# A fused transformer layer on one core: a scale for each half of a pair's activations, products reordered, the output projection pipelined and the late sums spread over ten rounds

## Chip, core and metric

The kernel runs on one core of a Trainium2 chip. The core has a matrix engine (TensorE, PE in the rows; its weight loads are PEld), three elementwise engines (VectorE or DVE, ScalarE or ACT, GpSimd or POOL) and a queue processor (SyncE or SP), which issues nearly all DMAs of this kernel in one order. Each engine runs its own instructions in order and waits on semaphores for the others. The metric is the device time of one execution in microseconds, lower is better; the figure compared is the median of several runs.

## The reference, cut to what matters

One layer (DEPTH is 1) on 2048 tokens of width 1024, all in float32:

```
h  = RMSNorm(x) * (1 + scale1(c)) + shift1(c)
u  = h @ W_in                                  # columns split among head groups
A, B = forgetting attention (8 heads x 64), differential attention (4 heads x 128)
x  = x + gate1(c) * (concat(A, B) @ W_out)
h2 = RMSNorm(x) * (1 + scale2(c)) + shift2(c)
x  = x + gate2(c) * ((silu(h2 @ w_gate) * (h2 @ w_up)) @ w_down)     # hidden width 2816
```

## The kernel before, in words

Float32 products are made of three float16 products: each operand is scaled by a power of two and split into a high and a low half (a cast on ACT, then the difference on DVE), and high*high, high*low and low*high are added in PSUM. The scale comes from a maximum over the tile: `absmax` on DVE gives one value per row, `colmax` spreads it over the rows by a small matmul on PE (line 108) and a second DVE maximum, and `pow2` makes scale and inverse in four short DVE instructions.

**First stage.** The 16 blocks of 128 tokens are normalised (`first_norm`), transposed on PE (`first_hT`) and projected. Per block the norm is a square with sum on ACT, an `rsqrt` of two ACT and three DVE instructions on one column, and a scaling on POOL.

**Attention** for eight head groups, with the input projection of the next group between its steps.

**Output projection.** `out_proj(blk)` loads x and the mixed heads of a block, splits them into `mh`, turns them by a DMA transpose into `mT` (two buffers), multiplies (2 x 24 matmuls), adds x and stores the row in DRAM (`x1d`). Blocks 0 to 9 stand between attention steps; blocks 10 to 15 come after the first gate weights were prepared.

**The gated layer.** Tokens are handled in two halves of 1024, hidden units in 11 pairs of 128, so there are 22 rounds `q`. Gate and up products go by a Strassen scheme: seven products (`product`, in the order `ORDER`) for each of gate (w = 0) and up (w = 1), 12 matmuls each (line 1091), 168 in a round. Their right side is one of seven sums of blocks of the normed tokens (`comb(i)`); `BSUM` says which blocks. The sums of the first half of the tokens (pairs 0 to 3) are made by `norm_sum` during the attention. Those of the second half (`jj` = 4 to 7, seven each, 28 in all) are made in rounds 2, 4, 6 and 8: `norm_load` and `norm_row` bring in and norm two rows, and then for each of the seven sums POOL adds (line 984), ACT casts (988), DVE subtracts (989), SP transposes (995) and stores to DRAM (996). Each sum takes one of the three `stage()` buffers, which the `w_down` loads use too.

After a round, `act` (both token halves `th` of the pair, 2048 values in a row) gets one scale in `act_scale`, and `act_split` makes `aT`. The 16 `down` products of round q (6 matmuls each, line 1149, 96 in all) run in round q+1, as `DOWNAT` spreads them over its 14 slots; DVE adds each to x (line 1153). A slot is one product, its downs, and then whatever steps the code put there.

At a product's end the sums of Strassen's scheme are made from PSUM by DVE, POOL and ACT. For the last (`i` = 6, w = 1):

```
V.tensor_tensor(out=tmp, in0=b, in1=tmp, op=ALU.add)                     # 1120
G.tensor_tensor(out=tmp, in0=tmp, in1=dif, op=ALU.add)                   # 1125
G.tensor_tensor(out=act[:, 1, 1], in0=tmp, in1=act[:, 1, 1], op=ALU.mult) # 1126
```

and `act_scale` of the next round waits for it. A scheduler orders the instructions of each engine from this program, so that steps move a few slots against the text.

## Time and profile before

| | |
|---|---|
| runs | 2935.83, 2925.38, 2928.06 us; median 2928.06 |
| profiled execution | 2939.51 us, its span 2937.7 us |
| PE busy | 2728.9 us, 93% of the span |
| DVE, POOL, ACT busy | 72%, 55%, 49% of the span |
| mean granted clock of PE | 0.98 of full speed |

The profiled execution is 11.4 us longer than the median of the runs, so differences worked out from its rows are taken off the median. Rounds are counted on PE by line 1091: each has 168 of its matmuls. Round 1 begins at 1631.83 us, round 3 at 1753.93, round 10 at 2200.66, round 13 at 2387.92 and round 21 at 2845.55.

### The profile page before, as it was taken

What the parts mean: (1) busy time and instruction counts of PE and PEld (TensorE: products, weight loads), DVE (VectorE), ACT (ScalarE), POOL (GpSimd) and SP (SyncE); (2) the same over time, 40 slices, a digit from 0 to 9 for tenths busy, and PEclk for the clock granted to TensorE, in tenths of its full rate; (3) what the DMA queues carried; (4) which work ended last, traced back from release to release, by engine and by line L of the source; (5) the groups of instructions that cost most, each with busy time, mean ns of one, the idle gap of its engine ahead of it and who ended that gap; (6) DMA issues with size and microseconds to landing.
All of it is one profiled execution on the core that took longest, in us unless ns stands there. A gap on an engine that the chain in (4) does not pass through costs nothing.

```text
span 2937.7 us, 49384 instructions
## 1 busy us (share of the span) xinstructions
PE 2728.9 (93%) x18902; PEld 1479.9 (50%) x18902; DVE 2111.3 (72%) x4077; ACT 1441.2 (49%) x2725; POOL 1609.5 (55%) x1392
## 2 busy tenths in 40 slices
PE   5789989899999999999989998899999999999998
PEld 3456656566665655664444343444444444444443
DVE  7786675857758686656744887787878778778775
ACT  4666667666676777786543422333323332233230
POOL 2566666665667787675542645444545444535430
PEclk9899999999999999999999999999999999999999
DMA  6232231322224233234776223224234511112101
GB/s 230 77 82 61 63 73 39 82 53 67 73 50 94 53 105 95 49 103 118 171 196 202 85 68 98 72 79 110 70 108 150 165 59 57 58 52 64 58 22 58
DMA packets 269902, 261.92 MB, mean 89 GB/s; under 512 B 204376, under 2 KB 221144, under 8 KB 263904
## 3 DMA queue, kind: packets, MB, share of 16 engines
q1 hardware_dynamic: 269664, 258.75, 31.0%
q8 instruction: 148, 2.42, 0.4%
q14 instruction: 90, 0.74, 0.1%
HBM read 173.55 MB, written 36.91 MB: 72 GB/s over the span
## 4 chain that ended last, share of the span: by engine, by line
PE 52%; DVE 21%; DMA 12%; POOL 6%; ACT 6%; issue 4%; SPq 0%; POOLq 0%; DVEq 0%; ACTq 0%
PE ps_mx L1149 10%; PE ps_ip L437 10%; PE ps_st L1091 7%; PE ps_pv L1091 6%; DMA stg<-in_w_ada_dram 3%; PE ps_ip L934 3%; DMA stg<-stg 2%; PE ps_mx L1091 2%; PE ps_st L579 2%; DVE t_mxc L548 2%; PE ps_st L580 2%; PE ps_pv L609 2%; PE ps_mx L546 2%; PE ps_pv L608 2%; PE ps_pv L607 2%
## 5 line engine op out<-in xcount | busy, mean ns | idle before, releaser
L593 POOL TENSOR_TENSOR pxs<-pxs 128x512 f16<-128x512 f32 (+3 forms) x640 | 683.3, 1082 | 325.8 <-ACT pxs L590 191.8
L1091 PEld LDWEIGHTS <-mt 128*128 128x128 f16 x3696 | 361.8, 99 | 446.7 <-issue 22.0
L437 PE MATMUL ps_ip<-wbuf,ht 128*128 128x384 f16 (+1 forms) x2952 | 560.6, 332 | 26.1 <-DVE vts L144 13.5
L1149 PE MATMUL ps_mx<-wide,ht 128*128 128x512 f16 x2112 | 505.4, 382 | 11.5 <-ACT ht L139 5.6
L1038 POOL TENSOR_TENSOR pxm<-vts 128x512 f32<-128x512 f32 x220 | 295.7, 1370 | 347.1 <-DMA vts<-in_w_gu_dram 316.3
L585 ACT ACTIVATE pxs<-ps_st,cells 128x512 f32<-128x512 f32 (+3 forms) x640 | 388.7, 619 | 142.5 <-PE ps_st L580 68.9
L437 PEld LDWEIGHTS <-ht 128*128 128x128 f16 x3072 | 295.7, 99 | 243.5 <-issue 46.2
L1091 PE MATMUL ps_st<-ht,mt 128*128 128x512 f16 x1584 | 383.0, 386 | 5.6 <-ACT mt L1094 3.2
L1091 PE MATMUL ps_pv<-ht,mt 128*128 128x512 f16 x1584 | 383.3, 380 | 1.1 <-ACT mt L1096 1.1
L590 ACT ACTIVATE pxs<-pxs 128x512 f16<-128x512 f32 (+3 forms) x640 | 350.7, 565 | 16.4 <-PE ps_pv L609 7.6
L607 PE MATMUL ps_pv<-vts,pxs 128*128 128x129 f16 (+1 forms) x2176 | 342.6, 207 | 4.2 <-DVE os L626 3.1
L608 PE MATMUL ps_pv<-vts,pxs 128*128 128x128 f16 (+1 forms) x2176 | 344.7, 208 | 0.0
L1149 PEld LDWEIGHTS <-ht 128*128 128x128 f16 x2112 | 206.3, 98 | 266.7 <-issue 16.9
L609 PE MATMUL ps_pv<-vts,pxs 128*128 128x129 f16 (+1 forms) x2176 | 325.6, 207 | 9.8 <-POOL pxs L593 8.9
L548 DVE TENSOR_REDUCE t_mxc<-ps_mx 128x1 f32<-128x512 f32 x384 | 256.9, 682 | 93.8 <-PE ps_mx L546 92.0
L1153 DVE SCALAR_TENSOR_TENSOR mt<-ps_mx,t_ai,mt 128x512 f32<-128x512 f32 x352 | 256.6, 743 | 75.5 <-PE ps_mx L1149 75.2
L607 PEld LDWEIGHTS <-pxs 128*128 128x128 f16 x2176 | 208.2, 97 | 56.7 <-ACT pxs L585 3.5
L579 PE MATMUL ps_st<-mt 67*128 67x512 f16 (+7 forms) x640 | 223.8, 350 | 10.4 <-ACT pxs L585 10.2
L609 PEld LDWEIGHTS <-pxs 128*128 128x128 f16 x2176 | 206.8, 99 | 50.0 <-POOL pxs L593 24.3
L608 PEld LDWEIGHTS <-pxs 128*128 128x128 f16 x2176 | 208.0, 97 | 35.3 <-issue 4.1
L580 PE MATMUL ps_st<-mt 128*128 128x512 f16 (+3 forms) x640 | 223.8, 350 | 0.0
L546 PE MATMUL ps_mx<-mt 71*128 71x512 f16 (+7 forms) x640 | 197.3, 350 | 19.6 <-DVE t_mxc L548 13.1
(266 smaller groups left out, 4097.0 us busy)
## 6 DMA issues: line engine op xcount, KB each, us to landing
vts<-in_w_gu_dram SPq DMA_DIRECT2D x44, 1024.0 KB
stg<-in_w_down_dram SPq DMA_DIRECT2D x44, 512.0 KB
stg<-in_w_ada_dram SPq DMA_DIRECT2D x32, 512.0 KB
stg<-in_w_in_dram SPq DMA_DIRECT2D x24, 512.0 KB
mt<-in_w_ada_dram SPq DMA_DIRECT2D x16, 512.0 KB
mt<-mt SPq DMA_DIRECT2D x128, 64.0 KB
mixed<-os SPq DMA_DIRECT2D x32, 256.0 KB
stg<-in_w_out_dram SPq DMA_DIRECT2D x16, 512.0 KB
```

The costliest lines, as they stand in the source:

```text
L437: T.matmul(pt[:, 0:N], lhsT=h4[:, k, hs, c : c + P], rhs=w4[k // 4][:, k % 4, ws, 0:N], start=(i == 0), stop=(i == len(terms) - 1))
L548: V.tensor_reduce(out=mx[:, 4 * j + n : 4 * j + n + 1], in_=b[:, 0:w], op=ALU.max, axis=AX.X)
L579: T.matmul(b[:, c0:QC], lhsT=K2[0:K, kb * P : (kb + 1) * P], rhs=QA[0:K, q0:q1], start=True, stop=False, skip_group_check=True)
L585: A.activation(p32[:, c0:QC], b[:, c0:QC], AF.Exp, bias=pshift, scale=1.0)
L590: A.activation(ph[:, c0:QC], p32[:, c0:QC], AF.Copy, bias=0.0, scale=1.0)
L593: (V if hilo[1] == "V" else G).tensor_tensor(out=pl[:, c0:QC], in0=p32[:, c0:QC], in1=ph[:, c0:QC], op=ALU.subtract)
L607: T.matmul(pv[:, jj, :], lhsT=lhs_h, rhs=v4[:, kb, h, 0 : W + 1], start=first, stop=False, skip_group_check=True)
L608: T.matmul(pv[:, jj, 0:W], lhsT=lhs_h, rhs=v4[:, kb, h, W + 2 : 2 * W + 2], start=False, stop=False, skip_group_check=True)
L609: T.matmul(pv[:, jj, :], lhsT=lhs_l, rhs=v4[:, kb, h, 0 : W + 1], start=False, stop=end, skip_group_check=True)
L1038: G.tensor_tensor(out=sums[:, k * 512 : (k + 1) * 512], in0=raw[:, a * 512 : (a + 1) * 512], in1=raw[:, b * 512 : (b + 1) * 512], op=op)
L1091: T.matmul(b.rearrange("p (b n) -> p b n", b=4), lhsT=aw[w][:, APOS[i] * 4 + k, ws, :], rhs=cb[:, :, 2 * k + hb, :], start=(fresh and k == ...
L1149: T.matmul(b, lhsT=aT[:, th, as_, f, j * P : (j + 1) * P], rhs=dnb[:, (2 * q + f) % 4, ws, n * 512 : (n + 1) * 512], start=(f == 0 and z = ...
```

## The change

`act_scale` and `act_bound` work per half `th`: two maxima over 1024 values in a row, two colmax matmuls, two pow2. In `ORDER` product 7 comes ahead of 3, so that half 0 of `act` is whole after product 7 of w = 1; its bound, scale and split stand in slots 11 to 13 of the same round, those of half 1 in slots 0 to 2 of the next, and `DOWNAT` begins in slot 1. POOL's sum `tmp + dif` moves ahead of the last product. In the output projection the load of the next block and its split go ahead of a block's second half. The gate weights' first steps are cut up among blocks 10 to 15. The second half's tokens are normed right after their output block (`late_row`, stored in `yd`), and each of the 28 sums becomes five steps on their own slots (`late_sum`), three sums a round in rounds 0 to 9, with their blocks loaded from `yd`. In the first stage the squares of four blocks share one rsqrt.

```diff
+    def first_stats(c, r4):
+        ss = small(4, "dss", bufs=2)
+        for j in range(4):
+            A.activation(sqs.bitcast(F16), xcs[c][:, j, :], AF.Square, bias=0.0, scale=1.0, accum_out=ss[:, j : j + 1])
+        V.tensor_scalar(out=ss, in0=ss, scalar1=1.0 / D, scalar2=EPS, op0=ALU.mult, op1=ALU.add)
+        r = small(4, "drr", bufs=2)
+        rsqrt(ss, r, 4)
+        r4["r"] = r
+    def first_scale(blk, r4):
+        xt = xcs[blk // 4][:, blk % 4, :]
+        G.tensor_scalar(out=xt, in0=xt, scalar1=r4["r"][:, blk % 4 : blk % 4 + 1], scalar2=0.0, op0=ALU.mult, op1=ALU.add)
...
-        rows = [(0, lambda: hts.append(htile()))]
+        rows = [(0, lambda: hts.append(htile())), (2, lambda: first_stats(c, r4))]
         for j in range(4 * c, 4 * c + 4):
-            rows.append((1, lambda j=j: first_norm(j)))
+            rows.append((0.5, lambda j=j: first_scale(j, r4)))
...
     def out_proj(blk):
         if blk == 0:
             hs.extend(htile() for _ in range(4))
+            out_load(0)
+            out_split(0)
...
+        if blk + 1 < NB:
+            out_load(blk + 1)
         for n in range(2):
...
+            if n == 0 and blk + 1 < NB:
+                out_split(blk + 1)
         nc.sync.dma_start(x1d[blk], x1)
...
+        if blk > 8:
+            late_row(blk - 1)
...
-    ORDER = (4, 5, 1, 2, 3, 7, 6)
+    ORDER = (4, 5, 1, 2, 7, 3, 6)
...
+    def late_row(blk):
+        y = pairbuf(blk // 2)[:, blk % 2, :]
+        norm_rows2(y, blk)
+        nc.sync.dma_start(yd[blk - 8], y)
+    def late_sum(jj, i):
+        (za, ha), op, other = BSUM[i]
+        st = {}
+        def load():
+            e = st["e"] = stage()
+            for c, (z, h) in enumerate([(za, ha)] + ([other] if other else [])):
+                nc.sync.dma_start(e[:, c * 512 : (c + 1) * 512], yd[2 * jj - 8 + z][:, h * 512 : (h + 1) * 512])
...
+        def add():
+            e = st["e"]
+            if other:
+                G.tensor_tensor(out=e[:, 0:512], in0=e[:, 0:512], in1=e[:, 512:1024], op=op)
+            s3, hi, _, _ = parts()
+            A.activation(hi, s3, AF.Copy, bias=0.0, scale=1.0)
+        def low():
+            s3, hi, lo, _ = parts()
+            V.tensor_tensor(out=lo, in0=s3, in1=hi, op=ALU.subtract)
+        def turn():
+            tr = st["e"][:, 0:512].bitcast(F16)
+            nc.sync.dma_start(tr.rearrange("p (k n) -> p k n", n=P), parts()[3], transpose=True)
+        def store():
+            nc.sync.dma_start(hcd[ORDER.index(i), jj - 4], st["e"][:, 0:512].bitcast(F16))
+        return [(0, load), (2, add), (3, low), (4, turn), (5, store)]
...
         elif i == 3:
             V.tensor_tensor(out=dif, in0=b, in1=dif, op=ALU.subtract)
+            G.tensor_tensor(out=tmp, in0=tmp, in1=dif, op=ALU.add)
...
             V.tensor_tensor(out=tmp, in0=b, in1=tmp, op=ALU.add)
             if w == 0:
-                G.tensor_tensor(out=act[:, 1, 1], in0=tmp, in1=dif, op=ALU.add)
-                A.activation(act[:, 1, 1], act[:, 1, 1], AF.Silu, bias=0.0, scale=gi)
+                A.activation(act[:, 1, 1], tmp, AF.Silu, bias=0.0, scale=gi)
             else:
-                G.tensor_tensor(out=tmp, in0=tmp, in1=dif, op=ALU.add)
                 G.tensor_tensor(out=act[:, 1, 1], in0=tmp, in1=act[:, 1, 1], op=ALU.mult)
...
-    def act_scale(q):
+    def act_bound(q, th):
+        sets[q]["aam", th] = absmax(act[:, th], BF16, axis=AX.XY)
+    def act_scale(q, th):
...
-    run(outs[10:16])
+    run(outs[14:16])
+    late_row(15)
...
-    DOWNAT = (0, 0, 0, 0, 2, 2, 2, 2, 2, 2, 1, 1, 1, 1)
+    DOWNAT = (0, 1, 1, 1, 1, 1, 2, 1, 1, 2, 2, 2, 1, 0)
...
+    late = [[] for _ in range(14 * (NQP + 1))]
+    for k, steps in enumerate([late_sum(jj, i) for jj in range(4, 8) for i in ORDER]):
+        for d, f in steps:
+            late[14 * (k // 3) + (6, 9, 13)[k % 3] + d].append(f)
...
+        if q < NQP:
+            at(11, act_bound, q, 0)
+            at(12, act_scale, q, 0)
+            at(13, act_split, q, 0)
         if q:
-            at(0, act_scale, q - 1)
-            at(1, act_split, q - 1, 0)
+            at(0, act_bound, q - 1, 1)
+            at(1, act_scale, q - 1, 1)
             at(2, act_split, q - 1, 1)
...
-                for _ in range(DOWNAT[slot]):
+                for _ in range(DOWNAT[slot] if q < NQP else (3, 2, 2, 1, 8)[slot] if slot < 5 else 0):
```

Three places of the built order show how it comes out. The first is POOL at the end of the up half of round 2, before the change: L984 is a late sum's add, L1118 the multiply that ends half 0, L1125 and L1126 the last two steps of half 1, L1038 the sums of the next gate or up weights, L1097 a step of product 5.

```order
674 L984 TENSOR_TENSOR stg<-stg 128x512
675 L1118 TENSOR_TENSOR uhm<-mt,uhm 128x512
676 L1038 TENSOR_TENSOR pxm<-vts 128x512 x3
677 L1097 TENSOR_TENSOR mt<-mt 128x512
678 L984 TENSOR_TENSOR stg<-stg 128x512
679 L1125 TENSOR_TENSOR pxm<-pxm,wide 128x512
680 L1038 TENSOR_TENSOR pxm<-vts 128x512 x2
681 L1126 TENSOR_TENSOR uhm<-pxm,uhm 128x512
682 L984 TENSOR_TENSOR stg<-stg 128x512 x2
```

After the change, at the end of a round with late sums (L1043 is now the add, L1183 the multiply of half 0, L1173 `tmp + dif`, L1189 the multiply of half 1, L1127 a `w_down` step, L1162 the step of product 5):

```order
676 L1162 TENSOR_TENSOR mt<-mt 128x512
677 L1043 TENSOR_TENSOR stg<-stg 128x512
678 L1127 TENSOR_TENSOR stg<-stg,grep_21994 128x1024
679 L1183 TENSOR_TENSOR uhm<-mt,uhm 128x512
680 L1173 TENSOR_TENSOR pxm<-pxm,wide 128x512
681 L1043 TENSOR_TENSOR stg<-stg 128x512
682 L1189 TENSOR_TENSOR uhm<-pxm,uhm 128x512
683 L1100 TENSOR_TENSOR pxm<-vts 128x512 x5
```

The weights' sums have left the way between the last steps of half 1, but an add of a late sum still stands right ahead of L1189.

The second place is DVE at the end of the program, before: one maximum L123 over both halves after the last product's L1120, one scale (t_as), both splits (L144), and then the 16 adds of the downs.

```order
3740 L1120 TENSOR_TENSOR pxm<-ps_mx,pxm 128x512
3741 L1153 SCALAR_TENSOR_TENSOR mt<-ps_mx,t_ai,mt 128x512
3742 L123 TENSOR_REDUCE t_amh<-uhm 128x1
3743 L109 TENSOR_REDUCE t_cm<-ps_ip 128x1
3744 L115 TENSOR_SCALAR t_p2a<-t_cm 128x1
3745 L116 TENSOR_SCALAR t_as<-t_p2a 128x1
...
3749 L144 SCALAR_TENSOR_TENSOR ht<-uhm,t_as,ht 128x1024 x2
3750 L1153 SCALAR_TENSOR_TENSOR mt<-ps_mx,t_ai,mt 128x512 x16
```

After (L1185 is the last product's add, L1219 a down's):

```order
3899 L109 TENSOR_REDUCE t_cm<-ps_ip 128x1
...
3905 L1185 TENSOR_TENSOR pxm<-ps_mx,pxm 128x512
3906 L144 SCALAR_TENSOR_TENSOR ht<-uhm,t_as,ht 128x1024
3907 L123 TENSOR_REDUCE t_amh<-uhm 128x1
3908 L1219 SCALAR_TENSOR_TENSOR mt<-ps_mx,t_ai,mt 128x512 x3
3909 L109 TENSOR_REDUCE t_cm<-ps_ip 128x1
3910 L115 TENSOR_SCALAR t_p2a<-t_cm 128x1
```

Half 0's scale now stands ahead of the last product's add, and three downs run before half 1's scale.

The third place is SP at the end of the attention, before: L666 stores the last heads, L924 loads mixed rows of blocks 12 and on, L928 transposes a block.

```order
444 L1031 DMA vts<-in_w_gu_dram 128x2048
445 L666 DMA mixed<-os 128x4x128
446 L924 DMA stg<-mixed 128x1024 x3
447 L1174 DMA grep_22080<-grow 128x1024
448 L1179 DMA mt<-x1d 128x1024 x4
449 L924 DMA stg<-mixed 128x1024
450 L1031 DMA vts<-in_w_gu_dram 128x2048
451 L928 DMA_TRANSPOSE wide<-wide 128x16x128
```

After (L1093 gate weights, L680 the store, L938 the loads, L946 the transpose):

```order
445 L1093 DMA vts<-in_w_gu_dram 128x2048
446 L680 DMA mixed<-os 128x4x128
447 L969 DMA x1d<-ht 128x1024
448 L938 DMA stg<-mixed 128x1024 x3
449 L1244 DMA grep_21994<-grow 128x1024
450 L946 DMA_TRANSPOSE wide<-wide 128x16x128
```

The transpose of block 12 no longer stands behind four x1d loads and a second load of weights; the wait for L680 is where it was.

## Rows read from the trace of the kernel before

**Rows 1.** The page's first line.

```profile
span 2937.7 us, 49384 instructions
```

**Rows 2.** Stretches of whole rounds: length; busy us (instructions) by engine; granted clock; DMA share.

```profile
core 0: us, PE busy (x) PEld busy (x) DVE busy (x) ACT busy (x) POOL busy (x), PEclk, DMA share, GB/s
1631.83:1753.93 122.10, 114.28 (x515) 50.50 (x513) 107.17 (x150) 41.20 (x46) 67.90 (x41) 0.97 0.20 68
1753.93:2200.66 446.73, 410.56 (x1865) 182.54 (x1864) 345.98 (x495) 134.66 (x164) 228.07 (x146) 0.97 0.32 91
2200.66:2387.92 187.26, 181.70 (x835) 81.84 (x834) 148.16 (x215) 56.19 (x62) 86.86 (x57) 0.98 0.42 143
2387.92:2845.55 457.63, 457.63 (x2146) 208.08 (x2145) 359.05 (x527) 142.94 (x160) 212.29 (x144) 1.00 0.16 52
2845.55:2937.70 92.15, 81.92 (x370) 36.44 (x368) 49.07 (x72) 13.99 (x17) 10.99 (x9) 0.96 0.12 46
```

**Rows 3.** Line 1091 alone in one of these stretches: length, PE busy (matmuls).

```profile
2387.92:2845.55 457.63, 308.81 (x1346) 130.47 (x1345) 1.00 0.16 52
```

**Rows 4.** PE's waits from 1691 to 2388: total us, times, longest.

```profile
PE ps_ip L108 <- DVE t_amh L123: 29.0, 5, 7.3
```

**Rows 5.** POOL's waits in the same stretch.

```profile
POOL stg L984 <- DMA hcd<-stg: 101.0, 16, 11.0
```

**Rows 6.** Timeline of one stall in round 3: start, duration, idle time before in brackets.

```profile
1766.96 1.24 SPq L995 DMA_TRANSPOSE stg<-stg  x1
1770.91 0.32 SPq L996 DMA_DIRECT2D hcd<-stg  x1
1773.15 1.27 POOL L984 TENSOR_TENSOR stg<-stg 128x512 f32<-128x512 f32 x1 [5.08 <-DMA hcd<-stg]
1778.49 1.26 POOL L1126 TENSOR_TENSOR uhm<-pxm,uhm 128x512 f32<-128x512 f32 x1
1781.48 1.27 POOL L984 TENSOR_TENSOR stg<-stg 128x512 f32<-128x512 f32 x1 [1.73 <-DMA hcd<-stg]
1782.13 0.29 PE L108 MATMUL ps_ip<-idb,t_amh 128*128 128x128 bf16 x1 [7.32 <-DVE t_amh L123]
```

**Rows 7.** Groups from 1753 to 2200 by shape: count, busy us, mean ns, idle before.

```profile
L984 POOL TENSOR_TENSOR stg<-stg 128x512 f32<-128x512 f32 x19 | 28.2, 1484 | 101.0 <-DMA hcd<-stg 101.0
L974 DVE SCALAR_TENSOR_TENSOR stg<-stg,cells,vts 128x1024 f32<-128x1024 f32 x6 | 11.7, 1952 | 0.0
```

**Rows 8.** Groups from 2388 to 2845.

```profile
L109 DVE TENSOR_REDUCE t_cm<-ps_ip 128x1 f32<-128x128 f32 x32 | 9.1, 283 | 2.5 <-PE ps_ip L108 2.5
L118 DVE TENSOR_SCALAR t_p2b<-t_p2a 128x1 f32<-128x1 f32 x32 | 4.6, 144 | 0.0
```

**Rows 9.** Timeline after the last product.

```profile
2906.25 2.29 DVE L123 TENSOR_REDUCE t_amh<-uhm 128x1 bf16<-128x2048 f32 x1 [1.36 <-POOL uhm L1126]
2908.59 0.29 PE L108 MATMUL ps_ip<-idb,t_amh 128*128 128x128 bf16 x1 [4.50 <-DVE t_amh L123]
...
2910.88 23.08 PE L1149 MATMUL ps_mx<-wide,ht 128*128 128x512 f16 x96 [2.00 <-ACT ht L139]
```

**Rows 10.** Timeline at the end of the attention.

```profile
1529.71 0.33 SPq L1031 DMA_DIRECT2D vts<-in_w_gu_dram  x1
1530.65 0.95 SPq L666 DMA_DIRECT2D mixed<-os  x1
1538.30 1.28 SPq L924 DMA_DIRECT2D stg<-mixed  x3
1539.86 0.29 PE L108 MATMUL ps_ip<-idb,t_amh 128*128 128x128 bf16 x1 [7.37 <-DVE t_amh L123]
1541.68 1.15 ACT L139 ACTIVATE wide<-stg,cells 128x1024 f16<-128x1024 f32 x1 [13.55 <-DMA stg<-mixed]
```

**Rows 11.** PE's longest waits for a DMA from 1345 to 1530.

```profile
PE ps_ip L934 <- DMA wide<-wide: 5.7, 3, 2.3
```

**Rows 12.** PE's waits from 36 to 150.

```profile
PE ps_mx L108 <- DVE t_nr L135: 5.6, 1, 5.6
```

More of the change, by code (lines that the diff above doesn't have):

```diff
@@ L915, in pairbuf, with out_load, out_split @@
         return t.rearrange("p (b n) -> p b n", b=2)
-    def out_proj(blk):
-        if blk == 0:
-            hs.extend(htile() for _ in range(4))
-        x1 = pairbuf(blk // 2)[:, blk % 2, :]
-        rows = slice(blk * P, (blk + 1) * P)
-        nc.sync.dma_start(x1, t["x"][rows, :])
+    oin = {}
+    def out_load(blk):
         mt = stage()
-        nc.sync.dma_start(mt, mixed[rows, :])
+        nc.sync.dma_start(mt, mixed[blk * P : (blk + 1) * P, :])
+        oin[blk] = mt
+    def out_split(blk):
+        mt = oin.pop(blk)
         mh, mT = scr[:, 0], scr[:, 1 + blk % 2].rearrange("p s (k n) -> p s k n", k=KT)
@@ L1152, in down @@
         xs = xb[:, n * 512 : (n + 1) * 512]
-        V.scalar_tensor_tensor(out=xs, in0=b, scalar=sets[q]["ai"], in1=xs, op0=ALU.mult, op1=ALU.add)
+        V.scalar_tensor_tensor(out=xs, in0=b, scalar=sets[q]["ai", th], in1=xs, op0=ALU.mult, op1=ALU.add)
         if q % NPAIR == NPAIR - 1:
@@ L1165, in trunk @@
     gu_load(0, 0)
+    run(outs[10:11])
     gu_bound(0, 0)
```

80 lines of the change are left out of this document (39 added, 41 removed).

## The prediction

> **What bounds the kernel now.** I read the page's first line and the table of stretches first, then PE's and POOL's waits, then timelines around the longest waits. The span is 2937.7 us [rows 1]; the profiled execution with what lies around it took 2939.51, 11.4 more than the median 2928.06. I take differences out of the trace and off the median.
>
> The table [rows 2] holds the argument. From 2387.92 to 2845.55 eight whole rounds run, and PE is busy for 457.63 of 457.63 us at granted clock 1.00: 57.2 us a round, 0.213 us a matmul, and nothing to wait for. That is the price of a round when nothing is late. Against it the others have an excess: rounds 1 and 2, 122.10 - 2 x 57.2 = 7.7 us; rounds 3 to 9, 446.73 - 7 x 57.2 = 46.3; rounds 10 to 12, 187.26 - 3 x 57.2 = 15.7; the last round with its downs, 92.15 - 57.2 - 96 x 0.213 = 14.5. Of the 46.3, PE is idle for 446.73 - 410.56 = 36.2; the other 10.1 is matmuls that ran slower: the granted clock averages 0.97 there, and it falls to 1.2 GHz in pieces behind the stalls, so an idle microsecond costs about 10.1 / 36.2 = 0.28 more.
>
> The view of waits says for what: from 1691 to 2388 PE stands 29.0 us, in 5 stalls of up to 7.3, at the colmax matmul of line 108 for the maximum of `act` [rows 4]. Behind it is POOL, whose adds of late sums (L984) wait 101.0 us in 16 waits for the store of a stage buffer [rows 5]. The timeline shows one [rows 6]: the add of 1773.15 waited 5.08 us for the store issued at 1770.91, itself 3.95 us behind its transpose; only then POOL reaches L1126, 1778.49, and PE's colmax, at 1782.13, has been waited for 7.32 us. Adds come every 8.33 us, because each recycles the one buffer. So the kernel is PE-bound but for a queue on POOL in rounds 2 to 9 and three spots outside.
>
> **The change part by part.**
>
> *Late sums, rounds 3 to 9: -39.* The add, cast, subtraction, transpose and store get slots of their own (some 4 us each), three sums a round. The buffer that an add uses has been loaded two slots earlier, so the add no longer waits for a store issued just ahead. The weights' sums have left the way to L1189; one late add still stands there. If its data are in, it costs 1.48 us [rows 7] once a round, at most 7 x 1.48 = 10 in seven rounds. Against that stands slack: in the new order the colmax of half 1 lies three and a half products behind the last one. A product takes 12 x 308.81 / 1346 = 2.75 us [rows 3], so some 9 us, and the chain is an add (bounded by 1.48), a multiply of 1.26 [rows 6], and a maximum of half of 2.29 [rows 9], 3.9 us, or about 5 with DVE's queue. I give 1 us a round back: 46.3 - 7 = 39. Bounds: 46 (all hidden) and 0 (another wait takes its place).
>
> *Norm rows.* Eight rows of two DVE instructions, 1.95 us for the first [rows 7] and I take no more for the second, leave the rounds: up to 31 us off DVE there, put into the output projection with eight stores on SP. Nothing on PE waits for them until round 0's sums. Zero; the cover is PE's attention work.
>
> *Rounds 10 to 12: -9.* No sum is left there after the change; but the stretch also reloads `comb` from `hcd` (DMA share 0.42 [rows 2]), which stays, and 28 sums now end at round 9 instead of 8, closer to their use. I take somewhat over half of 15.7; bounds 0 and -15.7.
>
> *Rounds 1 and 2: 0.* They have 7.7 to give and receive sums that they hadn't (rounds 0 and 1 none, 2 seven). Bounds -7.7 and +8, one stall like rows 4's largest.
>
> *Half scales: +1.* Each round gains a colmax matmul, 0.29 us if PE is shown at it in order of time [rows 6], but 0.213 as an ordinary one: 21 x 0.22 = 4.6 at most, and the removed wait for the whole `act` covers much of it. On DVE it adds a maximum's second reading (0.28) and five scalings (0.144 each): 1.0 us a round [rows 8]. DVE is busy 359.05 / 8 = 44.9 of 57.2 us in a clean round [rows 2], so it is hidden behind PE.
>
> *Tail: -7.* Now PE waits 4.50 us for the maximum and 2.00 for the cast, and then the 96 matmuls take 23.08, or 2.6 more than at 0.213 [rows 9]: 9.1 in all. In the new order half 0 is split ahead of the last product's add, and its eight downs (8 x 6 x 0.213 = 10.2 us) cover half 1's chain of 3.9. What is left is some 1.5 us of wait and a bit of slow clock. Bounds -9 and -2.
>
> *Output projection: -4.* Blocks 0 to 9 have PE wait three times for a DMA transpose, 5.7 us together [rows 11]; loading and splitting one block earlier puts these ahead of half a block of matmuls. I take two thirds. Bounds: -10 with the slow clock and other waits, +4 if the split, now between other DVE work, delays attention.
>
> *End of the attention: 0.* There PE idles 7.37 us ahead of a colmax. The mixed rows were stored at 1530.65, behind the 1 MB gate load of 1529.71, are loaded at 1538.30 and cast at 1541.68 [rows 10]. The change leaves store and load where they were in SP's order, and takes two loads from ahead of the transpose. But block 10 comes first and covers the colmax, while blocks 12 and on, which need those rows, now come sooner, with 60 matmuls (12.8 us) ahead. From 1529.7 that cover ends near 1542.5, and the cast of 1541.68, a subtraction and a transpose of about 4 us (as in rows 6) put the data near 1549: the idle time moves rather than goes. Bounds -9 (7.37 x 1.28) and +5.
>
> *First stage: -2.* PE waits once, 5.6 us, for the rsqrt's result of a block [rows 12]; four blocks now share one. But the first of them waits for four squares instead of one. Bounds -10 and +6.
>
> **Sum.** -39 - 9 + 0 + 1 - 7 - 4 + 0 - 2 = **-60**. The profiled execution would come out at 2879.5, the median at 2928.06 - 60 = **2868**.
>
> **Rivals.**
>
> *Everything is hidden.* All the excess of rounds 1 to 12 goes, 69.7, with 9.1 of the tail and 5.7 of the projection: -84.5, 2843.5. For it: the clean rounds show that PE waits for nothing when POOL is on time. Against it: POOL still has an add ahead of L1189. 18 in 100.
>
> *The sums hold their buffers.* A sum keeps a stage buffer for five slots, some 20 us; three a round and two `w_down` steps share three buffers. If a load waits for a buffer, SP, which issues in order, holds all weight loads behind it. Then a stall of 29.0 / 5 = 5.8 us [rows 4] in seven of ten rounds comes back, 41 us: 2909. For it: the 101.0 us of rows 5 are exactly waits for buffers. Against it: 3 x 20 + 2 x 25 = 110 of 3 x 57.2 = 172 us of buffers. 10 in 100.
>
> *The end of the attention gets worse.* With blocks 12 to 15 pulled ahead, each may wait for its mixed rows: two more waits of 7.37 with 0.28 behind each, 19 us: 2887. 7 in 100.
>
> *VectorE becomes the bound.* The new small operations, 1.0 us a round and a bit of fixed cost, 22 x 1.2 = 26 us, would then be paid in full: 2894. Against it: in the clean rounds PE has no idle time while DVE is busy 78% [rows 2]; for it, nothing but that share. 4 in 100. The Trainium skill (Perfetto Trace Analysis, Identifying the Most-Contended Engine) wants TensorE's headroom judged by MFU and weight-load busy time rather than by matmul busy time; weight loads fill 208.08 / 457.63 = 45% here, and by that rule DVE with 78% would be the most contended engine and additions to it would count. The row, with no gap on PE, speaks against it here.
>
> *Slower: the add ahead of L1189 waits.* If the late add that stands right ahead of L1189 finds its load from `yd` not landed, or its buffer held, L1189 waits with it, as L1126 does now, but in ten rounds instead of some four: 10 x 6 x 1.28 = 77 us on top of -60, 2945. It decides from 60 / 10 = 6 us in each of the ten rounds. Against it: two slots (8 us) lie between load and add, the SP queue is lightly used in clean rounds (DMA share 0.16 [rows 2]), and the slack is about 5 us, so the add would have to be 11 us late every round. 6 in 100.
>
> **How the numbers follow.** My forecast has 55 in 100, the rivals 45. The forecast's own bounds, mostly those of the 46.3 and the 15.7, are some 2850 to 2888. Reaching to 2842 takes in the case in which everything is hidden, and to 2906 the attention's end, VectorE and part of the buffers; about 2 in 10 lie outside: range 2842 to 2906. A run of this kernel tells about 0.5% (14.6 us) from no change. Faster by that, below 2913.4: forecast, everything hidden, attention's end, VectorE, and a little of the buffers' case, 0.87. Slower, above 2942.7: the add's case, 0.06. Between them: the rest, 0.07.
>
> **What would show it.** Right, if in the changed trace rounds 3 to 9 take 400 to 410 us with a clock near 1.00, POOL's late adds no longer wait for `hcd`, PE's waits at line 108 for `act` fall from 29.0 to under 8, the last stretch is near 85, and the pause at the end of the attention is still there at block 12 or so. Wrong, if POOL's late adds wait for loads from `yd`, if PE waits at line 108 in every round, if SP is late with weights in rounds 0 to 9, or if the rounds without sums (10 and on) no longer fill PE.

## The result and the profile after

The changed kernel took 2949.08 us (median of 5 runs, 2939.52 to 2950.74) against 2928.06: 1.0059 of the time before, 95% interval 1.0037 to 1.0081. It is slower by some 0.6% (the medians alone differ by 0.7%), where -60 us and 2868 were forecast.

The first line of its page has the same span as before [rows 1], although the medians are 21 us apart:

```profile
span 2937.7 us, 49754 instructions
```

The execution profiled of before was slower than its runs in the table ahead, that of the changed kernel as fast as the fastest of its own; a second trace of each comes with the experiments. The changed kernel's table of stretches, in whole rounds and with the columns of [rows 2]: rounds 1, 2, 3 to 9, 10 to 12, 13 to 20, and 21 with its downs.

```profile
1628.63:1690.51 61.88, 54.85 (x253) 24.08 (x252) 57.69 (x89) 23.86 (x27) 45.53 (x27) 1.00 0.42 128
1690.51:1765.31 74.80, 64.29 (x289) 28.14 (x288) 54.23 (x82) 18.71 (x24) 32.43 (x21) 0.98 0.32 93
1765.31:2222.79 457.48, 417.52 (x1885) 184.05 (x1884) 344.88 (x533) 134.60 (x159) 226.67 (x141) 0.97 0.29 88
2222.79:2396.09 173.30, 172.25 (x808) 78.23 (x807) 139.68 (x220) 53.94 (x60) 87.90 (x54) 1.00 0.44 146
2396.09:2854.58 458.49, 458.24 (x2154) 208.86 (x2152) 367.22 (x584) 144.58 (x160) 239.89 (x143) 1.00 0.17 55
2854.58:2937.70 83.12, 78.59 (x365) 35.22 (x363) 49.81 (x86) 14.11 (x17) 10.82 (x7) 1.00 0.13 51
```

Rounds 10 to 12 and 21 gained 14.0 and 9.0 us. Rounds 13 to 20 stand at 57.3 us each. Rounds 3 to 9 *lost* 10.7 and rounds 1 and 2 lost 14.6, with the clock still at 0.97. The changed kernel's waits from 1690 to 2223 us, rounds 2 to 9 (us in total, times, longest), say that the old stall is gone and others have come:

```profile
ACT stg L1045 <- POOL stg L1043: 123.2, 16, 12.0
...
POOL stg L1043 <- DMA stg<-yd: 68.0, 11, 10.2
DVE stg L1049 <- ACT stg L1045: 64.0, 19, 7.1
...
POOL uhm L1189 <- DVE pxm L1185: 18.9, 6, 4.3
...
PE ps_mx L1215 <- DVE mt L1219: 16.4, 12, 3.6
...
PE ps_mx L1215 <- ACT ht L139: 8.5, 5, 4.9
...
PE ps_mx L1156 <- DVE mt L1219: 6.8, 3, 4.1
...
PE ps_mx L1215 <- DVE t_ai L119: 5.3, 1, 5.3
...
PE ps_ip L108 <- DVE t_amh L123: 0.2, 1, 0.2
```

The 29.0 us at the colmax of `act` [rows 4] fell to 0.2. A late sum's steps wait one behind the other: POOL's add for its load, ACT's cast for the add, DVE's subtraction for the cast. The chain itself is not new. In the kernel before, from 1690 to 2223 us, it reads:

```profile
ACT stg L988 <- POOL stg L984: 89.4, 16, 8.2
...
DVE stg L989 <- ACT stg L988: 44.5, 12, 5.3
```

New is that it starts from a load instead of a store, and that ACT and DVE wait longer in it. DVE does its work in order, so what stands behind a waiting subtraction (L1219, the downs' adds; the scales of `act`) comes later; PE now waits for a down's bank, for half 0's split and for its scales. SP's own waits in the changed kernel from 1625 to 2225 us show what the loads stand behind:

```profile
SPq L1093 <- DVE mt L144: 194.8, 12, 25.0
SPq L1122 <- DVE wide L144: 71.6, 12, 9.4
...
SPq L1033 <- DMA hcd<-stg: 27.5, 17, 1.7
```

SP waits 194.8 us to issue gate weights (L1093) until their one buffer has been split, 71.6 to issue down weights (L1122), and 27.5 to issue a sum's load (L1033) until a stage buffer has been stored. The first of these is no cause by itself: in the same stretch the kernel before has as much, and the kernel without sums (no_sums, below), in which PE hardly waits, more than twice that:

```profile
SPq L1031 <- DVE mt L144: 197.8, 16, 29.8
SPq L1093 <- DVE mt L144: 456.9, 22, 26.5
```

One stall of the changed kernel in time order, from its timeline (start, duration, idle time before in brackets):

```profile
2023.90 0.80 SPq L1033 DMA_DIRECT2D stg<-yd  x2
...
2029.02 1.27 POOL L1043 TENSOR_TENSOR stg<-stg 128x512 f32<-128x512 f32 x1 [6.61 <-DMA stg<-yd]
...
2030.31 0.63 ACT L1045 ACTIVATE stg<-stg 128x512 f16<-128x512 f32 x1 [12.01 <-POOL stg L1043]
...
2030.98 0.69 DVE L1049 TENSOR_TENSOR stg<-stg 128x512 f16<-128x512 f32 x1 [6.48 <-ACT stg L1045]
...
2037.52 0.68 DVE L1185 TENSOR_TENSOR pxm<-ps_mx,pxm 128x512 f32<-128x512 f32 x1
...
2038.28 2.23 POOL L1189 TENSOR_TENSOR uhm<-pxm,uhm 128x512 f32<-128x512 f32 x1 [4.35 <-DVE pxm L1185]
...
2041.66 1.15 ACT L139 ACTIVATE ht<-uhm,t_as 128x1024 f16<-128x1024 f32 x1 [6.69 <-DVE t_as L116]
...
2042.73 0.14 DVE L119 TENSOR_SCALAR t_ai<-t_p2b 128x1 int32<-128x1 int32 x1
...
2042.86 0.54 PE L1215 MATMUL ps_mx<-wide,ht 128*128 128x512 f16 x1 [5.31 <-DVE t_ai L119]
```

The load goes out at 2023.90, behind no weights but behind the store of another sum (SP's row ahead, L1056 at 2021.88); POOL has been waiting for it for 6.61 us at 2029.02, and DVE stands 6.48 us at the subtraction; half 0's scale and split, which the change had brought forward, come out late behind it, and PE stands 5.31 us.

### The profile page after: what moved, and what is told of

Read it like the earlier page. It is cut to its first block, busy times and chain, and to the rows that moved or that the text cites. A ratio compares the mean times of both kernels' runs of the same rounds, so it can differ in the third digit from the quotient of the medians.

```text
span 2937.7 us, 49754 instructions
## 1 busy us (share of the span) xinstructions
PE 2725.0 (93%) x18924; PEld 1479.3 (50%) x18924; DVE 2149.6 (73%) x4195; ACT 1437.9 (49%) x2704; POOL 1655.1 (56%) x1392
## 4 chain that ended last, share of the span: by engine, by line
PE 47%; DVE 20%; DMA 16%; POOL 6%; ACT 5%; issue 5%; SPq 1%; POOLq 0%; DVEq 0%; ACTq 0%
PE ps_ip L451 9%; PE ps_mx L1215 8%; PE ps_pv L1156 6%; PE ps_st L1156 6%; DMA stg<-in_w_ada_dram 3%; DMA stg<-stg 2%; DMA vts<-in_w_gu_dram 2%; PE ps_ip L964 2%; POOL pxm L1100 2%; DVE t_mxc L562 2%; PE ps_mx L1156 2%; PE ps_st L593 2%; PE ps_st L594 2%; DVE mt L144 2%; PE ps_pv L623 2%
## 5 line engine op out<-in xcount | busy, mean ns | idle before, releaser
L1156 PEld LDWEIGHTS <-mt 128*128 128x128 f16 x3696 | 359.6, 98 | 445.5 <-issue 26.4
L1100 POOL TENSOR_TENSOR pxm<-vts 128x512 f32<-128x512 f32 x220 | 336.3, 1560 | 193.2 <-DMA vts<-in_w_gu_dram 175.0
L1156 PE MATMUL ps_st<-ht,mt 128*128 128x512 f16 x1584 | 375.6, 381 | 1.2 <-ACT mt L1159 0.6
L1156 PE MATMUL ps_pv<-ht,mt 128*128 128x512 f16 x1584 | 370.9, 381 | 0.0
L1219 DVE SCALAR_TENSOR_TENSOR mt<-ps_mx,t_ai,mt 128x512 f32<-128x512 f32 x352 | 256.6, 742 | 33.1 <-PE ps_mx L1215 33.0
L593 PE MATMUL ps_st<-mt 67*128 67x512 f16 (+7 forms) x640 | 223.6, 350 | 12.1 <-ACT pxs L599 11.8
L139 ACT ACTIVATE mt<-pxm,t_ws 128x1536 f16<-128x1536 f32 x88 | 118.8, 1357 | 197.8 <-DVE t_p2b L118 126.1
```

The costliest lines, as they stand in the source:

```text
L593: T.matmul(b[:, c0:QC], lhsT=K2[0:K, kb * P : (kb + 1) * P], rhs=QA[0:K, q0:q1], start=True, stop=False, skip_group_check=True)
L1100: G.tensor_tensor(out=sums[:, k * 512 : (k + 1) * 512], in0=raw[:, a * 512 : (a + 1) * 512], in1=raw[:, b * 512 : (b + 1) * 512], op=op)
L1156: T.matmul(b.rearrange("p (b n) -> p b n", b=4), lhsT=aw[w][:, APOS[i] * 4 + k, ws, :], rhs=cb[:, :, 2 * k + hb, :], start=(fresh and k == ...
```

## The experiments

Ratios are to the kernel before, run on the same chip, with 95% intervals. "Rounds 1 to 9" is the time from the first matmul of round 1 to that of round 10.

| kernel | median us | ratio | rounds 1 to 9, us |
|---|---|---|---|
| before (its two traces) | 2926 to 2931 | 1 | 568.8, 566.6 |
| changed | 2949.1 | 1.0059 (1.0037 to 1.0081) | 594.2 |
| late_only | 2946.2 | 1.0057 (1.0036 to 1.0079) | 580.3 |
| old_sums | 2921.8 | 0.9979 (0.9966 to 0.9991) | 574.9 |
| low_later | 2944.1 | 1.0040 (1.0022 to 1.0058) | 593.2 |
| before_again | 2929.3 | 0.9998 (0.9982 to 1.0014) | 566.6 |
| no_load | 2938.3 | 1.0024 (1.0014 to 1.0034) | 579.9 |
| act_only | 2943.2 | 1.0041 (1.0026 to 1.0056) | 584.1 |
| loads_act | 2940.4 | 1.0036 (1.0022 to 1.0050) | 592.7 |
| half_only | 2922.1 | 0.9965 (0.9952 to 0.9978) | 577.0 |
| no_sums | 2858.3 | 0.9759 (0.9740 to 0.9778) | 521.9 |
| own_buf | 2903.6 | 0.9913 (0.9892 to 0.9934) | 561.1 |
| out_only | 2929.3 | 1.0004 (0.9993 to 1.0016) | 570.3 |
| first_only | 2929.9 | 0.9991 (0.9976 to 1.0006) | 567.2 |
| own_tied | 2885.4 | 0.9860 (0.9840 to 0.9880) | 538.7 |
| no_rows | 2856.4 | 0.9769 (0.9744 to 0.9793) | 518.7 |
| tied_stage | 2908.9 | 0.9930 (0.9903 to 0.9957) | 555.6 |
| tied_late | 2900.0 | 0.9892 (0.9874 to 0.9910) | 552.4 |

### Which part does the harm

**late_only**: the kernel before with the late rows and late sums alone.

```diff
-        if q in (2, 4, 6, 8):
-            ...
-            for f in st[slot]:
+            for f in late[14 * q + slot] + st[slot]:
                 f()
```

> The kernel before with one part of the change: the late rows and the 28 late sums as five steps on slots of their own in rounds 0 to 9. Half scales, product order, output projection and first stage stay as before. Theory L (the late sums' chain does the harm: SP's loads come late, POOL, ACT and DVE each wait in line for the step ahead, and DVE's adds of the downs stand behind the waiting subtraction, so PE waits for a down's bank): rounds 1 to 9 take 585 to 605 us against 568.8 in the trace before, DVE waits some 50 us or more at the subtraction, and the median is 10 to 30 us above 2928. Rival H (the half scales with the new order of products and downs do the harm; the downs now start in slot 1 and share the bank of product 6): rounds 1 to 9 fall to 540 to 560, the median is 2900 to 2925.

**old_sums**: the changed kernel with `late_row` and `late_sum` taken out and the block `if q in (2, 4, 6, 8)` put back.

> The changed kernel with one part undone: the 28 late sums are made as before, seven each in rounds 2, 4, 6 and 8, from rows loaded and normed there; all else is as changed. Theory L: rounds 1 to 9 fall from 594.2 us in the changed kernel's trace to 555 to 575, PE's waits for a down's bank (DVE's add of it) from 16 us to under 6, and the median is 20 to 40 us below the changed kernel's 2949. Rival H: rounds 1 to 9 stay at 585 to 600 and PE still waits for the down's bank; the median is 2940 to 2955.

**low_later**:

```diff
-        return [(0, load), (2, add), (3, low), (4, turn), (5, store)]
+        return [(0, load), (3, add), (5, low), (6, turn), (7, store)]
```

> The changed kernel with the late sum's steps further apart: add three slots after the load instead of two, subtraction two slots after that instead of one, transpose and store each a slot later by as much (3, 5, 6, 7 for 2, 3, 4, 5). Theory L with too little distance as its root: DVE's waits at the subtraction fall from 64 us to under 30, rounds 1 to 9 to 565 to 580, the median to 2925 to 2938. If instead the three stage buffers are the root, a buffer is held longer and SP's loads come later still: rounds 1 to 9 at 595 to 620, median 2950 to 2970. Rival H: no change, 2945 to 2953.

**before_again**: the kernel before, unchanged.

> The kernel before once more, for a second trace of it: its first profiled execution took 2939.51 us where its runs have a median of 2928.06, while the changed kernel's took 2939.52 with a median of 2949.08. If the runs' difference of 21 us lies in the rounds with sums, whose waits differ from execution to execution, rounds 1 to 9 in this trace differ from the 568.8 us of the first by up to 11; if in the DMA-bound start, the first stage does. The ratio should be 1.000 within 0.003.

The late sums alone make the kernel before 17 us slower, and putting the old ones back makes the changed kernel 27 us faster (22 against its second measurement, low_later). So the new late sums do most of the harm, and rival H falls as the main cause. The mechanism of theory L is not shown by this. PE's waits for a down's bank were to fall from 16 us to under 6 in old_sums; from 1690 to 2223 us they stand at

```profile
PE ps_mx L1184 <- DVE mt L1188: 22.5, 21, 2.3
```

and in half_only (below), which has the old sums too, at

```profile
PE ps_mx L1167 <- DVE mt L1171: 18.2, 18, 2.1
```

against 3.0 in the kernel before and 12.1 in late_only. Either part of the change brings this wait, and the changed kernel's 16.4 can't be put down to the late sums alone. The rise in late_only's rounds 1 to 9 (580.3) was under the 585 foretold; the rest lies ahead of them, from block 0's first matmul of the output projection to round 1: 297.6 us against 283 to 286.

low_later told something else than it was made for. The order that it was built into is that of the changed kernel, row for row on all five engines: moving its steps by one or two slots changed nothing. So it is a second measurement of the changed kernel (2944.1), and the slots in the program are not slots on the chip.

before_again gives the trace that the first comparison lacked: 2927.9 us of span. Of the 9.8 us by which the first was longer, 6.6 lie ahead of the 614th matmul of the input projection and 6.0 in rounds 3 to 12, while the attention was shorter. Against the repeat of the changed program (span 2944.7), the gap of 16.8 is -0.2 in the start, +3.5 in the attention, +7.9 from block 0 to round 1, +12.2 in rounds 1 and 2, +14.4 in rounds 3 to 9, -12.6 in rounds 10 to 12, +0.7 in rounds 13 to 20, and -9.0 in round 21. Rounds 1 and 2, and 3 to 9, of before_again:

```profile
1627.18:1750.14 122.96, 113.47 (x514) 50.37 (x513) 106.57 (x150) 41.10 (x46) 67.64 (x41) 0.97 0.21 68
1750.14:2193.76 443.62, 408.79 (x1865) 182.48 (x1864) 346.16 (x496) 134.68 (x164) 227.21 (x146) 0.97 0.32 92
```

and of low_later:

```profile
1638.32:1773.47 135.15, 117.43 (x540) 51.87 (x539) 109.89 (x164) 41.82 (x50) 77.89 (x47) 1.00 0.37 109
1773.47:2231.53 458.06, 417.69 (x1885) 184.38 (x1884) 346.28 (x539) 135.50 (x159) 227.20 (x141) 0.97 0.28 88
```

### Which step of a late sum

**no_load**: no loads from `yd`; adds, casts and subtractions read a tile that is always there, so the sums' values are others (the diff is cut to the add).

```diff
-            for c, (z, h) in enumerate([(za, ha)] + ([other] if other else [])):
-                nc.sync.dma_start(e[:, c * 512 : (c + 1) * 512], ...)
-                G.tensor_tensor(out=e[:, 0:512], in0=e[:, 0:512], in1=e[:, 512:1024], op=op)
+                G.tensor_tensor(out=e[:, 0:512], in0=mod[:, 0:512], in1=mod[:, 512:1024], op=op)
```

> The changed kernel with the late sums' loads from DRAM left out: the adds, casts and subtractions take their data from a tile that is always there, so the sums' values are others. Transposes and stores stay. Theory L1 (the loads come late, and POOL's add waits for them, then ACT's cast, then DVE's subtraction): POOL's wait at the late add falls from 68 us to under 25, DVE's at the subtraction from 64 to under 30, rounds 1 to 9 from 594 us to 560 to 578, the median to 2915 to 2930. Rival L2 (the buffers and the transposes and stores behind them set the pace; loads are no worse than those): rounds 1 to 9 at 585 to 597, median 2940 to 2950, and POOL waits for the store instead. Rival L3 (the engines' time for the sums itself): as L2, but without these waits.

**act_only**: no add on POOL, no subtraction on DVE.

```diff
-                G.tensor_tensor(out=e[:, 0:512], in0=e[:, 0:512], in1=e[:, 512:1024], op=op)
+            A.activation(lo, s3, AF.Copy, bias=0.0, scale=1.0)
-            V.tensor_tensor(out=lo, in0=s3, in1=hi, op=ALU.subtract)
```

> The changed kernel with POOL's add and DVE's subtraction of each late sum left out (ACT writes both halves by two casts, so the sums' values are others); loads, transposes and stores stay, and so do ACT's waits. Theory L1 (what costs PE its time is that DVE's adds of the downs and POOL's multiply stand in line behind a waiting step of a sum): PE's waits for a down's bank fall from 24 us to under 8, rounds 1 to 9 from 594 us to 555 to 575, the median to 2910 to 2930. Rival L4 (the DMAs themselves, in SP's queue and on the DMA engines, make the weights late): rounds 1 to 9 at 583 to 597 and the median at 2938 to 2952, with POOL's sums of weights still waiting some 46 us for their load.

**loads_act**:

```diff
-                nc.sync.dma_start(e[:, c * 512 : (c + 1) * 512], yd[...])
+                nc.scalar.dma_start(e[:, c * 512 : (c + 1) * 512], yd[...])
```

> The changed kernel with the 48 late loads issued from ACT's queue instead of SP's, where they stand behind gate weight loads that wait 195 us in all for their buffer. Theory L1 with SP's queue as the root: POOL's wait at the late add falls from 68 us to under 40, rounds 1 to 9 to 570 to 585, the median to 2925 to 2940. If the stage buffers are the root, the load waits on ACT for the buffer instead, and ACT's casts stand behind it: rounds 1 to 9 at 590 to 615, median 2945 to 2970.

**half_only**: the kernel before with half scales, product order, downs and last round alone, and with the new slots of the down weights (see below).

> The kernel before with the gated layer's part of the change alone: half scales, product order, places of the downs, the sum of product 3 taken ahead, the last round's downs. Late sums, output projection and first stage as before. The kernel with late sums undone took 2921.8 against 2929.4. If the gated part gives all of that and the first stage and output projection together give nothing: 2919 to 2925, tail 79.4 us against 88.4, rounds 1 to 9 near 575 against 567 to 569. If the output projection and first stage gave some 5 us of it: 2925 to 2931. If they cost: 2912 to 2919.

None of the three single steps is the cause by itself. Without loads, rounds 1 to 9 keep 58 us over the price without sums (521.9), between the branches of the expectation, and POOL's add waits for a buffer's store instead. With POOL and DVE left out of the sums, ACT takes over the waiting, and PE now waits for ACT. Issuing the loads from ACT shortens POOL's wait and gains nothing in rounds 1 to 9 (592.7). Their waits from 1690 to 2223 us, first no_load's:

```profile
POOL stg L1041 <- DMA hcd<-stg: 42.1, 10, 9.6
```

act_only's:

```profile
ACT stg L1043 <- DMA stg<-yd: 153.7, 21, 9.4
...
PE ps_mx L1213 <- ACT ht L139: 27.2, 6, 5.2
```

and loads_act's:

```profile
POOL stg L1043 <- DMA stg<-yd: 37.1, 8, 10.1
```

So it isn't DVE as such: in act_only it is ACT that meets a sum's data before they are there and holds up what stands behind it. The theory as act_only's expectation had it, that DVE and POOL are the place, fell; so did SP's queue as the only root. act_only's times (584.1 and 2943.2) are those of its rival L4, the DMAs themselves; but no row of PE's waits there names the weights, and tied_late, below, makes the same transfers in 42 us less than the changed kernel.

half_only gains 8 us, as much as old_sums: 9 in the tail and 8 in rounds 10 to 12 (176.4 against 184.4), and loses 8 to 10 in rounds 1 to 9, where the wait for a down's bank grew from 3.0 to 18.2. In it and in the changed kernel the load of the down weights also moves from slots 3 and 4 to 1 and 2 and their split from 9 and 10 to 6 and 7, which shifts the time in which they hold stage buffers; no run takes that apart.

### What the sums cost, and the two small parts

**no_sums**: the changed kernel without late sums and reload.

```diff
-            for f in late[14 * q + slot] + st[slot]:
+            for f in st[slot]:
-                if q == NPAIR - 1 and w == 1:
-                    ...
```

> The changed kernel with the 28 late sums left out altogether, and with them the reload of the combined tokens, so that the second half of the tokens is multiplied with the first half's sums; the late rows are still normed and stored. If the sums are all that keeps rounds 1 to 9 from the price of a clean round (57.3 us), these take 516 to 522 us against 594 in the changed kernel, and the median falls to 2858 to 2880. If the half scales or the weights' own loads and buffers cost there too, rounds 1 to 9 take 530 to 560 and the median is 2885 to 2920. The output projection with round 0, 294 us from block 0 to round 1 in the changed kernel against 283 to 286 before, falls to 283 to 288 if the sums of round 0 cost there, and stays at 291 to 296 if it is the late rows' norm and stores.

**own_buf**:

```diff
-            e = st["e"] = stage()
+            k = (jj * 7 + ORDER.index(i)) % 2
+            e = st["e"] = mod[:, k * 1024 : (k + 1) * 1024]
```

> The changed kernel with two buffers of their own for the late sums, in the tile of the modulation rows, which is free by then; the three stage buffers are left to the down weights. If the sharing of stage buffers sets the pace (a load on SP waits for a store or for the split of down weights, and gate weights stand behind it), POOL's and DVE's waits at late steps fall below 40 us each from 68 and 64, rounds 1 to 9 from 594 to 560 to 580, the median to 2912 to 2935. If it is the latency of a sum's own chain (load, add, cast, subtraction, transpose, store, each on another in-order engine), which more buffers don't shorten: 583 to 597, 2938 to 2952.

**out_only** and **first_only**: the kernel before with the new `out_proj` and cut-up gate weights alone, and with `first_stats` and `first_scale` alone.

> The kernel before with the output projection's part of the change alone: the next block's load and split ahead of a block's second half, and the gate weights' first steps cut up among blocks 10 to 15. The prediction gave it -4 us and the end of the attention 0. The changed kernel's trace shows the waits for transposes in blocks 0 to 9 replaced by as many for DVE's add in the same bank, and one of 11.2 us for a transpose in place of the 7.4 at line 108. If so: no gain, 2926 to 2934. If the prediction's term holds: 2922 to 2928. If the cut-up order costs: 2933 to 2942.

> The kernel before with the first stage's part of the change alone: the squares of four blocks share one rsqrt. The prediction gave it -2 us (-10 to +6). The traces so far have the 614th matmul of the input projection at 288.3, 281.6 and 280.8 us without it (the last in a kernel whose start is as before) and at 275.6 to 281.4 with it, which looks like some -3 us with as much scatter from run to run. If that is so: 2923 to 2929; if it is worth the 12 us of the first pair of traces: 2915 to 2921; if nothing: 2927 to 2932.

Without sums PE never waits from round 3 on (rounds 3 to 9 of no_sums, 57.3 us each):

```profile
1743.56:2144.37 400.81, 400.81 (x1885) 182.79 (x1883) 322.52 (x512) 126.76 (x140) 212.32 (x126) 1.00 0.17 56
```

So 594.2 - 521.9 = 72.3 us hang on the 28 sums, 2.6 us a sum. From round 3 on half scales, weights and buffers of the weights cost nothing by themselves; beside the old sums they cost the 8 to 10 us of half_only. (Round 1 takes 63.8 us even without sums.) Own buffers take 33 us away, and the median came out below the 2912 to 2935 expected. They also let the scheduler bunch the sums (3, 7, 12 and 6 in rounds 0 to 3), whose rounds 1 to 3 took 67, 81 and 70 us, and then every round is clean. The Trainium skill (Perfetto Trace Analysis, Optimization Strategy) says that a repeated gap on the engine that should be full can mean too few buffers for the next tile; own_buf agrees for 33 of the 72 us, in a run in which the order of the sums changed too. The output projection and the first stage measure as nothing.

### Buffers or order

**own_tied**: own buffers, and each load behind a product of its round.

```diff
-            e = st["e"] = stage()
+            k = jj * 7 + ORDER.index(i) - 28
+            e = st["e"] = mod[:, k % 2 * 1024 : (k % 2 + 1) * 1024]
+            src = (s5s, dif, tmp)[k % 3][:, 0:1]
+            A.activation(e[:, 0:1], src, AF.Copy, bias=0.0, scale=1.0)
+            if other:
+                A.activation(e[:, 512:513], src, AF.Copy, bias=0.0, scale=1.0)
...
-            late[14 * (k // 3) + (6, 9, 13)[k % 3] + d].append(f)
+            late[14 * (k // 3) + (1, 5, 9)[k % 3] + d].append(f)
```

> The changed kernel with two buffers of their own for the late sums, and each sum's load tied to a product of its round (a one-column copy on ACT from what products 5, 3 and 1 leave goes ahead of it into the buffer), so that the sums stay spread at three a round; in the run with own buffers alone the scheduler bunched all 28 in rounds 0 to 3, which cost there and left rounds 4 to 9 clean. If shared buffers are what made the spread sums dear, and spreading itself is sound: rounds 1 to 9 take 522 to 545 us (522 without any sums, 561 bunched, 594 as changed), median 2862 to 2888. If the chain of a sum over five in-order engines costs wherever it stands, some 2.6 us a sum: 570 to 597, 2912 to 2950.

**no_rows**: no_sums without `late_row` too.

> The changed kernel without late sums and reload, as in the run before, and without the late rows' norm and stores too. The output projection with round 0 took 293.7 us there, 294.4 as changed, and 283 to 289 in the kernels without late rows. If the rows cost some 6 us: 284 to 290, median 2849 to 2856. If they are hidden, as the prediction had it, and the difference is scatter: 291 to 296, median 2855 to 2861.

**tied_stage**: own_tied with `e = st["e"] = stage()`.

> The run with own buffers and ties, with one thing undone: the late sums share the three stage buffers with the down weights again, as in the changed kernel; the ties stay. This makes the table of two by two whole (ties or none, own buffers or shared). If the sharing is what costs: rounds 1 to 9 take 580 to 600 us (594 as changed, 539 with own buffers and ties), median 2935 to 2955. If the ties do the work and buffers little: 535 to 560, median 2880 to 2910.

**tied_late**: tied_stage with the ties elsewhere.

```diff
-            src = (s5s, dif, tmp)[k % 3][:, 0:1]
+            src = tmp[:, 0:1]
-            late[14 * (k // 3) + (1, 5, 9)[k % 3] + d].append(f)
+            late[14 * (k // 3) + (6, 9, 13)[k % 3] + d].append(f)
```

> The run with ties and shared stage buffers, with the ties moved to where the change had meant the loads: behind products 6 and 1 (slots 6, 9 and 13 of a round) instead of 5, 3 and 1 (slots 1, 5 and 9). If the place in the round made the difference (the end of a round, where the last sums of the act and the second gate load stand): rounds 1 to 9 take 580 to 600 us, median 2930 to 2955. If it is the tie itself, which keeps each load from being issued and its steps from being put in line before their time: 548 to 570, median 2900 to 2922.

Rounds 1 to 9 in us, 521.9 without sums:

| | no ties | ties |
|---|---|---|
| shared stage buffers | 594.2 | 555.6 (tied_late 552.4) |
| own buffers | 561.1 | 538.7 |

Both count, and either alone gives over half of the 55.5 us that both give together; own buffers without ties also bunch the sums, so that cell changes more than the buffers. For tied_stage I had expected 580 to 600 if sharing was the cause; it came out on the other branch. tied_late, with the slots of the change and its shared buffers, differs from the changed kernel by the ties alone (the copies on ACT and the order that comes of them) and is 49 us faster, or 44 against the second measurement. Beside tied_stage's 555.6 it shows that the place in the round matters little, and that a step is bound to a place matters much. Nor is it the number of sums in a round: rounds 3, 4 and 7 have three subtractions in both kernels and took 65.7, 67.4 and 68.6 us as changed, 61.5, 61.5 and 59.6 in tied_late. Rounds 3 to 9 of tied_late:

```profile
1755.15:2183.71 428.56, 407.94 (x1885) 183.12 (x1884) 346.99 (x535) 139.10 (x195) 230.58 (x143) 0.99 0.31 101
```

of own_tied:

```profile
1754.78:2168.05 413.27, 402.89 (x1884) 182.68 (x1883) 342.42 (x532) 139.72 (x193) 224.31 (x141) 1.00 0.32 99
```

and own_tied's wait at the subtraction from 1690 to 2223 us:

```profile
DVE vts L1054 <- ACT vts L1050: 27.6, 15, 3.5
```

PE's idle time in these seven rounds falls from 40.0 us to 20.6 and 10.4, the clock rises from 0.97 to 0.99 and 1.00, and DVE's wait at the subtraction from 64.0 to 27.6. PE's waits in tied_late from 1690 to 2223 us tell what the ties took away:

```profile
PE ps_mx L1220 <- DVE mt L1224: 20.5, 23, 2.9
...
PE ps_mx L1220 <- ACT ht L139: 0.2, 1, 0.2
```

The waits for half 0's split (8.5 us as changed), for its scale (5.3) and at L1156 for a down's add (6.8) fell to 0.2 in all. The wait for a down's bank, 16.4 as changed, stayed, and in own_tied it is 10.4. own_tied beats both kernels: 41 us below before, 64 below the change (59 below its second measurement). It still pays 16.8 us for its sums, 0.6 each.

no_rows leaves one thing open. From block 0 of the output projection to round 1 its trace takes 286.1 us, 7.6 less than no_sums's 293.7, but the medians are 1.9 us apart, with ratios whose intervals overlap.

## Why the prediction was wrong

**The step that failed** is the first and largest: "The add, cast, subtraction, transpose and store get slots of their own (some 4 us each)" and "has been loaded two slots earlier, so the add no longer waits". The slots are a wish of the program, and low_later shows that the scheduler gave the same order for others. On the chip the loads came late, and the add waited for them as it had for the store: 68.0 us in 11 waits after [rows 5] 101.0 in 16. Nor are the loads all of it: in no_load, without them, the add waits 42.1 us for a store, and rounds 1 to 9 take 579.9. Leaving the 28 chains out gives 72.3 us back, and buffers of their own with steps bound to their place 55.5; the prediction had 1 us a round for them. What PE waits for changed, not how long: the sign asked for at line 108, under 8 us, came true with 0.2, and rounds 3 to 9 were slower all the same. Of -39 for rounds 3 to 9 came +10.7, and of 0 for rounds 1 and 2 +14.6, outside the bound of +8, since the spread brought five sums into round 2.

**Late sums, second error.** I weighed one neighbour, the add ahead of L1189, and called 10 us its worst price. Its chain did have slack: L1189 waits for DVE, not for an add. But a sum has a step on SP, POOL, ACT and DVE each, and in the stall shown ahead the one that hurt was DVE's subtraction; act_only, which has none, loses nearly as much through ACT. The DMA share (0.16), by which I called the SP queue lightly used in clean rounds, says nothing of its waits: 456.9 us in no_sums. The rival "the add ahead of L1189 waits" came near the measured time (2945), by luck: the traces don't show its mechanism. (With its own factor of 1.28 it decides from 60 / 12.8 = 4.7 us a round, not 6.) The rival of held buffers named half of the cause; its 5.8 us in seven rounds gave 41, and the return was 39 + 25 = 64 over rounds 1 to 9. Own buffers give 33 us back without ties and 17 with them.

**The output projection (-4) and the first stage (-2)** measure 0 alone (1.0004 and 0.9991, both intervals across 1). The 5.7 us of [rows 11] went, but PE's waits in the changed kernel from 1331 to 1632 us show others in their place:

```profile
PE ps_ip L964 <- DMA wide<-wide: 11.0, 1, 11.0
PE ps_ip L964 <- DVE uhm L966: 6.5, 4, 2.5
...
PE ps_ip L964 <- DVE ht L966: 4.0, 2, 3.0
```

The 10.5 us of the lower two are for DVE's add into the bank that the next block wants (6.2 before, from 1345 to 1632 us). For the first stage [rows 12] was misread. The matmul that waits 5.6 us reads a maximum, not the rsqrt's result, and that maximum waited for a tile of input weights; the rsqrt only ended last. From the kernel before's timeline:

```profile
122.67 1.22 DVE L123 TENSOR_REDUCE t_amh<-stg 128x1 bf16<-128x1024 f32 x1 [3.29 <-DMA stg<-in_w_in_dram]
123.81 0.15 DVE L135 SCALAR_TENSOR_TENSOR t_nr<-t_rq,t_ry 128x1 f32<-128x1 f32 x1
...
123.95 0.29 PE L108 MATMUL ps_mx<-idb,t_amh 128*128 128x128 bf16 x1 [5.56 <-DVE t_nr L135]
```

The changed kernel, with one rsqrt for four blocks, still waits at such maxima from 36 to 150 us:

```profile
PE ps_mx L108 <- DVE t_amh L123: 7.4, 2, 4.0
```

**The end of the attention (0)** was right in kind: the 7.37 us of [rows 10] moved to a block's transpose, the 11.0 us of the first row (5.4 in out_only). **Norm rows (0)** are unsettled, as told under no_rows: between 2 by the medians and 8 by the trace.

**Right:** the clean round as price (no_sums has nothing else from round 3 on). The tail: -9.0 for -7, with PE's waits there now 0.5 and 0.2 us. Rounds 10 to 12: -12.6 to -14.0 for -9, but not shown to be for the reason given: half_only, with the old sums, gained 8 there, late_only, with the new sums alone, 10, and out_only, which has neither, 6. Half scales: 57.3 for 57.2 us a clean round, 0.1 x 22 = 2 us for 1; that the gated part would cost 8 to 10 us beside sums (half_only, rounds 1 to 9) was not in the term. VectorE did not become the bound: it is busy 367.22 of 458.49 us, 80%, in rounds in which PE is full; the traces bear out the row. The Trainium skill (Perfetto Trace Analysis, Identifying the Most-Contended Engine), cited ahead of the result, judges TensorE by MFU and by weight-load busy time; the prediction worked out only the second (45%) and left MFU out, so these rounds speak against that one-sided use and not against the page.

**Still open:** which effect of the ties does it (the loads' issue, their landing, or the order on the three engines), since the ties move all three; and why PE's loss (72.3, 30.5 and 16.8 us in the changed kernel, tied_late and own_tied) falls faster than DVE's wait at the subtraction (64.0, 42.6, 27.6; own_buf even loses 39.2 us with 17.7). That wait is no measure of the loss, and which queue carries how much of it is not shown.

## What to carry to other kernels

Work that is spread out to be hidden can add waits to every in-order engine that it touches: count a step's wait on each of them, and what stands behind it, not only on the one that waited before. Where a scheduler sets the order, a slot in the program is not a time: look whether moving a step changes the built order, and bind a step to work of its round by data if its place matters. Price such work by leaving it out: no_sums tells that 72 us hang on 28 sums, and own_tied that buffers of their own and a bound order are worth 55 of them. And put a stall's waiting instruction beside what it reads before naming its cause: [rows 12] named the instruction that ended last.

## What was not expected of the hardware

Two profiled executions of one program differ by 7 to 10 us: the same built order gave spans of 2937.7 and 2944.7, and the kernel before 2937.7 and 2927.9, 6.6 of it ahead of the 614th projection matmul. One trace of each kernel would have shown no difference at all.
